# Expert pairs with a gate riding along: loading the gate weights in pair 2, its bases by column halves, side work handed out by products

## The chip, the cores and the metric

One core of a Trainium2 chip runs the program. The metric is the device time of one execution in microseconds (us), the median of several; smaller is better. Engines are named as in the profile: PE is TensorE (PEld its weight loads), DVE is VectorE, ACT is ScalarE, POOL is GpSimd and SP is SyncE, which here only issues DMAs.

## The reference, cut to what matters

Two blocks run one after the other on 512 rows of 1024 numbers. The change lies in the end of the second one, an expert layer in which each of 16 experts takes its own best rows, and a gate that reads the sum which the experts leave in x:

```python
def expert_choice_ffn(h, w_router, w_gate, w_up, w_down):
    cap = EC_CAPACITY * S // N_EXPERTS                 # 64 rows for each expert
    aff = softmax(h @ w_router)
    gates, idx = lax.top_k(aff.transpose(0, 2, 1), cap)
    xe = h[bidx, idx]
    a = einsum('becd,edf->becf', xe, w_gate)
    b = einsum('becd,edf->becf', xe, w_up)
    ye = einsum('becf,efd->becd', silu(a) * b, w_down)
    return zeros_like(h).at[bidx, idx].add(ye * gates[..., None])

x = x + expert_choice_ffn(rms_norm(x, norm_ffn), w_router, w_gate, w_up, w_down)
g = sigmoid(rms_norm(x, norm_ple) @ w_ple_gate)
e = rms_norm(p @ w_ple_proj, norm_ple_post)
x = x + g * e
```

Each expert's three weights are 1024 by 2048 in float32, 24 MB, so 384 MB go through the core in this stage.

## The kernel before, in words

**Pairs and slots.** Experts go two at a time, one in each half of the PE array: eight pairs, 0 to 7, from about 1030 us to the end. Weights come in chunks of 1 MB (128 by 2048), 48 for a pair and 384 in all, in the order in which PE uses them. A pair is cut into 24 slots of two chunks. A slot is eight matmuls on 64 columns, each of which the profile shows as two records. Slots 0 to 15 make gate and up in four sections (ga, ua, L1698 and L1699), slots 16 to 23 the down product (yd, L1728 and L1729). I write slot 4.2 for slot 2 of pair 4.

**Buffers.** A chunk waits for a free buffer; SP issues its load (L1292) in order, so a load that waits holds all behind it. Buffers come from five groups: chy (5) and x16 (2) serve to the end, chr (6) until the pair RETIRE, chl (3) until the pair E_AT. From pair RETIRE on there are thus seven.

**Side work.** Beside the slots runs work that has its own small lists. `todo` holds generators, and `between()`, called behind each slot, lets `meanwhile(n)` take n steps from it, where n comes from the table PACE (1.9 steps a slot in pairs 3 to 5, say). The generators are:

- `spread`: adds the two experts' output into x, a scatter for each of four row tiles and two column halves (po<-ys, L1538; x is the tile xk in the trace, the add is L1646).
- `embedding` (pair E_AT = 1): loads w_pp and pT into two chr buffers (L1577, L1578) and makes p @ w_ple_proj, eight tiles of two products (pe).
- `gate_base(t, h)`: the gate's product of what x holds at that time, for row tile t and column half h: eight transposes (ptg), then eight products (pg) with the gate weights. A product is one call of `halves`, two matmuls.
- `gate_pair`: adds to the gate what a pair adds to x later. It makes the product of the pair's outputs with the gate weights (z, eight products for each column half that has a base), splits it in two (zs, by ACT and DVE, L333 and L334), and scatters it into those tiles of g that had a base by then (po<-zs).

So the later a tile gets its base, the fewer scatters follow, and a column half needs z only from its first base on. BASE lists the pair in which each base is made: t0, t1 for h0 in pair 3, t2, t3 in pair 4, t0, t1 for h1 in pair 5, then one in pair 6 and one in pair 7. All bases of a pair must have read x before the pair's own output goes into it (L1741); as generators they stand behind the pair before's spread.

**Gate weights.** `ple_loads()` runs when pair RETIRE begins: four loads of 1 MB on SP into chr buffers (L1564), and eight scalings on POOL (L1566).

**Routing of the next pair.** `route` has its own list: a matmul (bc, L1470), DVE operations, a gather of the next pair's rows by POOL (xg, L1478), a copy of the gate factors (gs on POOL, L1484), a scaling of the rows (xg on ACT, L1486), and transposes (pxt). `between` advances it by half a step a slot.

**Order.** A scheduler orders each engine's instructions by priorities; from pair HOLD = 4 on, what `between` hands out is pinned behind the last matmul of its slot (`issue_after`). Before that it may be moved.

Of the kernel before, what the change touches and what calls it, by code (L numbers as in the profile page):

```python
# [27 lines left out]
XV = 4  # L28
ADA_N = 1
PO = 10  # L30
PACE = [1.0, 1.0, 1.0, 1.9, 1.9, 1.9, 2.1, 2.2]
ROUTE_PACE = 0.5
HOLD = 4
ADDPE = [1, 3, 5, 6]
TBK = 7
RETIRE = 3

BASE = {3: [(0, 0), (1, 0)], 4: [(2, 0), (3, 0)], 5: [(0, 1), (1, 1)], 6: [(2, 1)], 7: [(3, 1)]}
E_AT = 1
ADA0 = 0  # L40
ADA_EVERY = 3
# [188 lines left out]
def _build(ctx, tc, nc, a, dbg, stop):  # L230
# [9 lines left out]
    def bcast(src, n, parts=128, off=0):  # L240
        return bass.AP(tensor=src.tensor, offset=src.offset + off, ap=[[0, parts], [1, n]])
# [15 lines left out]
    def ps(name, tag, bufs, shape=(128, 512)):  # L257
        tag = tag[1:] if tag[0] == "=" else TG[0].get(name, tag)
        return psp.tile(list(shape), FT, name=name, tag=tag, bufs=bufs)
# [1015 lines left out]
    for p_ in range(8):  # L1275
# [9 lines left out]
        BUFS = {"chy": 5, "chr": 6, "chl": 3, "hts": 1, "yy": 2, "x16": 2}  # L1285
    UNTIL = {"x16": 48 * 8, "chy": 48 * 8, "chr": 48 * RETIRE, "chl": 48 * E_AT}
    first = ["chy"] * 5 + ["chr"] * 2 + ["hts"] + ["chr"] * 4 + ["x16"] * 2 + ["chl"] * 3 + ["yy"] * 2
# [212 lines left out]
    todo = []  # L1500

    def meanwhile(n=1):
        while todo and n:
            try:
                next(todo[0])
                n -= 1
            except StopIteration:
                todo.pop(0)

    todo.append(first_route())  # L1510
    meanwhile(ROUTE0)
# [12 lines left out]
    def s2k(name, shape=(128, S)):  # L1524
        return mp.tile(list(shape), FT, name=name, tag="sg", bufs=2)

    def hl(src, y):
        split(src, y[:, 0], y[:, 1])
        return y

    def yy(name):
        return mp.tile([128, 2, 2, S], FR, name=name, tag="yy", bufs=2)
# [17 lines left out]
    def halves(out, w, x_, start, stop):  # L1550

        for h in range(2):
            c_ = slice(64 * h, 64 * h + 64)
            T.matmul(out[c_], w[:, c_], x_, start=start, stop=stop)  # L1554

    def slot(tag):
        return pools[tag].tile([128, 2048], FT, name="ch", tag=tag, bufs=BUFS[tag])
# [12 lines left out]
    def embedding():  # L1570

        e = ple["e"] = [t[:, D * i:D * i + D] for t in (slot("chl"), slot("chl")) for i in range(2)]
        rest = slot("chl")
        gpost, ple["xf"] = rest[:, 0:D], rest[:, D:].rearrange("p (f c) -> p f c", f=8)
        P.dma_start(gpost, bcast(a["g_post"], D))
        wpp, pT = slot("chr").rearrange("p (k c) -> p k c", k=2), slot("chr")
        SY.dma_start(wpp, a["w_pp"][0].rearrange("p (k c) -> p k c", k=2))  # L1577
        SY.dma_start(pT[:, 0:1024], a["pT"])  # L1578
        pT = pT[:, 0:1024].rearrange("p (k c) -> p k c", k=2)
        yield  # L1580
        se = mp.tile([128, 8], FT, name="se")
        for t in range(4):
            for h in range(2):
                c_ = slice(S * h, S * h + S)
                pe_ = ps("pe", "o", 2)
                for k in range(2):
                    halves(pe_, pT[:, k, 128 * t:128 * t + 128], wpp[:, k, c_], k == 0, k == 1)
                V.tensor_copy(e[t][:, c_], pe_)
                A.activation(s2k("sq"), pe_, AF.Square, accum_out=se[:, 2 * t + h:2 * t + h + 1])
                yield  # L1590
        re_ = mp.tile([128, 4], FT, name="re_")
        tc.keep_in_program_order(A.preload_act_table_set(LN_EXP))
        rstd_parts(se, re_, 2)
        for t in range(4):
            V.scalar_tensor_tensor(e[t], e[t], re_[:, t:t + 1], gpost, op0=OP.mult, op1=OP.mult)
# [18 lines left out]
    def gate_pair(pr, yts, ott, zl):  # L1614

        hs = [h for h in range(2) if any(c[1] == h for p_, l in BASE.items() if p_ <= pr for c in l)]
        zl += [ps("z", "o", 2) for _ in hs]
        at = [(n, y) for n, c in enumerate((4, 4) if pr < 7 else (4, 2, 2)) for y in range(c)]
        left = [list(range(8)) if h in hs else [] for h in range(2)]
        while left[0] or left[1]:  # L1620

            ready = [h for h in range(2) if left[h] and at[left[h][0]][0] < len(yts)]
            if ready:
                h = ready[0] if pr == 7 else max(ready, key=lambda h: (len(left[h]), -h))
                k = left[h].pop(0)
                halves(zl[h], yts[at[k][0]][:, at[k][1]], ple["wg"][k // 2][:, k % 2, S * h:S * h + S], k == 0, k == 7)
            whole[:] = [not l for l in left] if pr == 7 else whole
            yield
        if pr == 7:
            return  # L1630
        zs = yy("zs")
        for h in hs:
            y = hl(zl[h], zs[:, h])
            yield
            for t in range(4):
                if snap.get((t, h), 8) <= pr:
                    g_ = ple["g"][t][:, S * h:S * h + S]
                    V.tensor_tensor(g_, g_, scatter(y, ott, t), op=OP.add)
                    yield

    def spread(y, ott, q):

        yield
        for t in range(4):
            x_ = xt[:, t, S * q:S * q + S]
            V.tensor_tensor(x_, x_, scatter(y, ott, t), op=OP.add)  # L1646
            yield

    snap, pairs, whole = {}, [0], [False, False]
    owed, way = [0.0], [0.0]  # L1650

    def between(last):

        owed[0] += PACE[pairs[0]]
        n = int(owed[0])
        owed[0] -= n
        with ExitStack() as c_:
            if pairs[0] >= HOLD:
                c_.enter_context(tc.issue_after(last.ins))
            way[0] += ROUTE_PACE  # L1660
            if way[0] >= 1 and (pairs[0] or not todo):
                way[0] -= 1
                on_the_way()
            meanwhile(n)

    sx = mp.tile([128, 12], FT, name="sx")
    for pr in range(8):
# [5 lines left out]
        if pr < 7:  # L1673
            ways.append(route(pr + 1))
        if pr == RETIRE:
            ple_loads()
        if pr == E_AT:
            todo.append(embedding())
        todo += [gate_base(*c) for c in BASE.get(pr, ())]
        hts, flip = None, []  # L1680
# [34 lines left out]
        _, gs, ott = routed.pop(pr)  # L1715
        ys, yts, z = yy("ys"), [], []
        if pr >= min(BASE):
            todo.append(gate_pair(pr, yts, ott, z))
        for q in range(2):
            parts = 2 if last and q else 1  # L1720
            n = S // parts
            for part in range(parts):
# [10 lines left out]
                y = hl(yg, ys[:, q, :, n * part:n * part + n])  # L1733
                if pr >= min(BASE):
                    pt = ps("pty", "pt", 2)[:, 0:n]
# [4 lines left out]
                    yts.append(yt)  # L1740
                while any(c not in snap for c in BASE.get(pr, ())):  # L1741
                    meanwhile()
# [15 lines left out]
    for h in range(2):  # L1758
# [5 lines left out]
        for t in range(4):  # L1764
            c_, n = slice(S * h, S * h + S), 4 * h + t
# [35 lines left out]
```

## Time and profile before

| | us |
|---|---|
| median of three runs | 2066.95 (2062.79 to 2067.37) |
| the profiled execution | 2067.67 |
| its span in the trace | 2065.9 |
| PE busy | 1944.7 (94%) |
| first matmul of pair 1, 2 | 1133.60, 1259.40 |
| last matmul of pair 2, first of pair 3 | 1379.58, 1400.54 |
| first matmul of pair 4, 5, 6, 7 | 1515.30, 1640.70, 1774.15, 1899.17 |
| end of pair 7's slots | 2028.0 |

Starts count from the beginning of the span. The page gives busy shares in 40 slices of 51.6 us each; "windows" give the same for stretches that one names: start and end, length, then busy time (and instructions) of PE, PEld, DVE, ACT and POOL, PE's granted clock as a share of 2.4 GHz, the mean busy share of the DMA engines, and GB/s. In a "timeline" each line is one instruction or a run of like ones: start, length, engine, line, operation, tiles, and in square brackets the idle time of the engine before it and what ended it. "Lines" group instructions: busy time, mean ns of one record.

### The profile page before, as it was taken

The page shows a single profiled execution, that of the slowest core. Times are in us where ns is not written, and L with a number is a line of the kernel's source. Part 1 is how long each engine was busy: PE and PEld are TensorE (multiplying, and loading weights), DVE is VectorE, ACT ScalarE, POOL GpSimd, SP SyncE. Part 2 cuts the span into 40 slices and gives each one's busy share as a digit, 9 for nine tenths or more (in the row PEclk, how much of TensorE's full clock was granted, in tenths as well). Part 3 has the DMA queues.
Part 4 walks back from the last instruction along what each step waited for, and adds up shares of the span by engine and source line. Part 5 has one row for each costly group of instructions (what it writes and reads, how often), then busy time and mean ns, then how long its engine had stood idle before and what let it go on. Part 6 is the DMA issues. An engine that isn't in the chain of part 4 may idle for free.

```text
span 2065.9 us, 23336 instructions
## 1 busy us (share of the span) xinstructions
PE 1944.7 (94%) x9084; PEld 1090.8 (53%) x9084; DVE 769.5 (37%) x1662; ACT 591.2 (29%) x1144; POOL 126.8 (6%) x127
## 2 busy tenths in 40 slices
PE   7989999989999998999899988779899999999998
PEld 4667667768888887777533322222334333333333
DVE  4767767764444346766431111010011111120212
ACT  4755656643333334454211110000000000100013
POOL 1210201300100000001000000020000000000000
PEclk9999989989999999999899999999999999999999
DMA  7432213432322231223889899999999999999991
GB/s 307 124 122 78 93 62 123 138 92 92 122 102 93 102 114 55 92 77 110 343 354 420 357 419 420 420 420 399 421 419 416 410 384 388 393 403 410 412 379 47
DMA packets 94191, 523.20 MB, mean 253 GB/s; under 512 B 11405, under 2 KB 11829, under 8 KB 43136
## 3 DMA queue, kind: packets, MB, share of 16 engines
q1 hardware_dynamic: 88832, 500.47, 61.7%
q0 software_dynamic: 3904, 18.88, 2.4%
q10 hardware_dynamic: 1344, 2.35, 0.3%
q8 instruction: 72, 1.18, 0.2%
q14 instruction: 39, 0.32, 0.0%
HBM read 510.31 MB, written 4.27 MB: 249 GB/s over the span
## 4 chain that ended last, share of the span: by engine, by line
PE 76%; DMA 13%; DVE 5%; ACT 3%; issue 2%; POOL 1%; DVEq 0%; POOLq 0%; SPq 0%; ACTq 0%
DMA ch<-in_w_ue_dram 6%; PE ua L1698 6%; PE ga L1699 5%; PE ga L1698 5%; PE yd L1729 4%; PE yd L1728 4%; DMA ch<-in_w_de_dram 4%; PE z L1554 3%; PE pg L1554 3%; PE od L653 2%; PE ua L1699 2%; PE po L1538 2%; PE ag L328 2%; PE ag L329 2%; PE ag L330 2%
## 5 line engine op out<-in xcount | busy, mean ns | idle before, releaser
L1699 PE MATMUL ua<-ch,xe 128*64 128x512 f32 x512 | 231.0, 595 | 14.4 <-DMA ch<-in_w_ue_dram 14.4
L1729 PE MATMUL yd<-ch,hts 128*64 128x512 f32 (+1 forms) x544 | 232.8, 576 | 11.1 <-DMA ch<-in_w_de_dram 11.1
L1698 PE MATMUL ga<-ch,xe 128*64 128x512 f32 x512 | 240.8, 605 | 0.0
L1699 PE MATMUL ga<-ch,xe 128*64 128x512 f32 x512 | 234.1, 602 | 1.9 <-DMA ch<-in_w_ge_dram 1.8
L1728 PE MATMUL yd<-ch,hts 128*64 128x512 f32 (+1 forms) x544 | 233.9, 577 | 0.0
L1698 PE MATMUL ua<-ch,xe 128*64 128x512 f32 x512 | 233.2, 595 | 0.0
L321 DVE TENSOR_TENSOR wlo<-pan,whi 128x1024 fp32r<-128x1024 f32 x119 | 147.8, 1242 | 161.4 <-ACT whi L318 159.1
L318 ACT ACTIVATE whi<-pan 128x1024 fp32r<-128x1024 f32 x119 | 125.8, 1057 | 201.9 <-PE ag L329 85.4
L1709 DVE TENSOR_TENSOR sg<-sg,ua 128x512 f32<-128x512 f32 x32 | 22.0, 687 | 283.8 <-PE ua L1699 283.8
L1729 PEld LDWEIGHTS yd<-ch,hts 128*64 128x64 f32 x544 | 72.8, 138 | 88.7 <-issue 63.8
L1699 PEld LDWEIGHTS ga<-ch,xe 128*64 128x64 f32 x512 | 66.8, 138 | 89.4 <-issue 82.0
L1698 PEld LDWEIGHTS ua<-ch,xe 128*64 128x64 f32 x512 | 67.3, 137 | 85.9 <-issue 84.5
L1728 PEld LDWEIGHTS yd<-ch,hts 128*64 128x64 f32 x544 | 72.2, 138 | 66.0 <-issue 64.3
L1699 PEld LDWEIGHTS ua<-ch,xe 128*64 128x64 f32 x512 | 67.3, 137 | 68.8 <-issue 42.4
L356 POOL TENSOR_TENSOR ada_a<-ada_a,adw 128x512 f32<-128x512 f32 x56 | 79.2, 1415 | 377.7 <-ACT ada_a L353 269.0
L334 DVE TENSOR_TENSOR ys<-yg,ys 128x512 fp32r<-128x512 f32 (+1 forms) x17 | 12.5, 736 | 222.6 <-ACT ys L333 222.6
L1698 PEld LDWEIGHTS ga<-ch,xe 128*64 128x64 f32 x512 | 65.9, 138 | 55.3 <-issue 54.0
L1688 ACT ACTIVATE hts<-pth 128x512 f32<-128x512 f32 x32 | 19.1, 596 | 265.5 <-PE pth L1687 265.5
L1732 ACT ACTIVATE yg<-yd,gs 128x512 f32<-128x512 f32 (+1 forms) x17 | 11.3, 662 | 277.8 <-PE yd L1729 210.1
L1708 ACT ACTIVATE sg<-ga 128x512 f32<-128x512 f32 x32 | 19.1, 597 | 209.8 <-PE ga L1699 209.8
L1554 PE MATMUL pg<-ch 128*64 128x512 f32 x256 | 76.8, 613 | 2.4 <-POOL ch L1566 2.4
L328 PE MATMUL ag<-hTh,whi 128*128 128x512 f32 x176 | 70.9, 403 | 2.2 <-ACT hTh L425 2.2
(902 smaller groups left out, 3739.3 us busy)
## 6 DMA issues: line engine op xcount, KB each, us to landing
ch<-in_w_de_dram SPq DMA_DIRECT2D x128, 1024.0 KB, 11.6
ch<-in_w_ue_dram SPq DMA_DIRECT2D x125, 1024.0 KB, 11.4
ch<-in_w_ge_dram SPq DMA_DIRECT2D x120, 1024.0 KB, 11.1
pan<-in_w_up_dram SPq DMA_DIRECT2D x44, 512.0 KB, 3.4
adw<-in_ada_dram SPq DMA_DIRECT2D x64, 256.0 KB, 2.7
pan<-in_w_in_dram SPq DMA_DIRECT2D x24, 512.0 KB, 3.7
pan<-in_w_dn_dram SPq DMA_DIRECT2D x22, 512.0 KB, 3.4
adr<-in_ada_dram SPq DMA_DIRECT2D x8, 1024.0 KB, 10.6
```

Of the source, the lines that this page charges most:

```text
L318: A.activation(hi, raw, AF.Copy)
L321: eng.tensor_tensor(lo, raw, hi.bitcast(FT), op=OP.subtract)
L328: T.matmul(out, wh, xh, start=first, stop=False)
L329: T.matmul(out, wh, xl, start=False, stop=False)
L330: T.matmul(out, wl, xh, start=False, stop=last)
L356: P.tensor_tensor(ada_next[1], ada_next[1], w, op=OP.add)
L653: T.matmul(acc_[64 * par:64 * par + 64, 128 * i:128 * i + 128], v(kb, par)[:w], p_[par][:w, 128 * kb:128 * kb + 128], start=start and kb = ...
L1554: T.matmul(out[c_], w[:, c_], x_, start=start, stop=stop)
L1698: T.matmul(acc_[m][0:64], xe[:, kk, 0:64], wa[:, k], start=kk == 0, stop=kk == 7)
L1699: mm = T.matmul(acc_[m][64:128], xe[:, kk, 64:128], wb[:, k], start=kk == 0, stop=kk == 7)
L1728: T.matmul(yd[0:64], hts[:, kk, 0:64], wa[:, k_], start=kk == 0, stop=kk == 15)
L1729: mm = T.matmul(yd[64:128], hts[:, kk, 64:128], wb[:, k_], start=kk == 0, stop=kk == 15)
```

## The change

Four things. RETIRE goes from 3 to 2, so the gate weights load when pair 2 begins. BASE is spread over pairs 2 to 7: two h0 bases in pair 2, two in pair 3, then one h1 base in each of pairs 4 to 7. The steps get weights: a tile of the embedding counts 2, a product 1, a scatter 0.5, and a `gate_pair` step that finds nothing ready counts 0 and ends the handing out for that slot. The table PACE is replaced by a number computed for each pair: its products divided by 23, with 14 more in pair 7.

```diff
-PACE = [1.0, 1.0, 1.0, 1.9, 1.9, 1.9, 2.1, 2.2]
+PACE0 = [1.0, 1.0]
-RETIRE = 3
+RETIRE = 2
-BASE = {3: [(0, 0), (1, 0)], 4: [(2, 0), (3, 0)], 5: [(0, 1), (1, 1)], 6: [(2, 1)], 7: [(3, 1)]}
+BASE = {2: [(0, 0), (1, 0)], 3: [(2, 0), (3, 0)], 4: [(0, 1)], 5: [(1, 1)], 6: [(2, 1)], 7: [(3, 1)]}
     def meanwhile(n=1):
-        while todo and n:
+        while todo and n > 0:
             try:
-                next(todo[0])
-                n -= 1
+                c = next(todo[0])
+                if c == 0:
+                    return 0
+                n -= 1 if c is None else c
             except StopIteration:
                 todo.pop(0)
+        return min(n, 0)
...
+    pace = list(PACE0)
+    for p_ in range(len(PACE0), 8):
+        made = [c for q_, l in BASE.items() if q_ < p_ for c in l]
+        n = 9.0 * len(BASE.get(p_, ())) + 5.0 + 9.0 * len({h for _, h in made}) + 0.5 * len(made)
+        pace.append((n + (14.0 if p_ == 7 else 1.0)) / 23)
...
-        owed[0] += PACE[pairs[0]]
-        n = int(owed[0])
-        owed[0] -= n
+        owed[0] += pace[pairs[0]]
...
-            meanwhile(n)
+            owed[0] = meanwhile(owed[0])
```

The yields become `yield 2` in `embedding`, `yield 1 if ready else 0` in `gate_pair`'s products, and `yield 0.5` in its scatters and in `spread`.

On SP, in the loads of pair 1, this is the order before (w_pp and pT are the embedding's, the rest are chunks):

```order
L1292 DMA ch<-in_w_ge_dram 128x2048 x4
L1292 DMA ch<-in_w_ue_dram 128x2048 x4
L1292 DMA ch<-in_w_ge_dram 128x2048 x4
L1292 DMA ch<-in_w_ue_dram 128x2048 x2
L1577 DMA ch<-in_w_pp_dram 128x2048
L1578 DMA ch<-in_pT_dram 128x1024
L1292 DMA ch<-in_w_ue_dram 128x2048 x2
```

And on SP in the same place after, beginning with the same chunks:

```order
L1292 DMA ch<-in_w_ge_dram 128x2048 x4
L1292 DMA ch<-in_w_ue_dram 128x2048 x2
L1581 DMA ch<-in_w_pp_dram 128x2048
L1582 DMA ch<-in_pT_dram 128x1024
L1292 DMA ch<-in_w_ue_dram 128x2048 x2
```

The two loads have moved eight chunks forward; the pe products (not shown) go from slots 1.6 to 1.11 to slots 1.2 to 1.10.

On POOL, the scalings of the gate weights (L1566) and the routing of the pair that follows (L1478, L1484) before, between pairs 2 and 3:

```order
L1566 TENSOR_TENSOR ch<-ch,cols 128x1024 x2
L1478 DMA xg<-xd,at 128x1056
L1566 TENSOR_TENSOR ch<-ch,cols 128x1024 x2
L1484 COPY gs<-xg 64x1 x2
L1566 TENSOR_TENSOR ch<-ch,cols 128x1024 x4
```

And on POOL after, now between pairs 1 and 2:

```order
L1570 TENSOR_TENSOR ch<-ch,cols 128x1024 x4
L1478 DMA xg<-xd,at 128x1056
L1570 TENSOR_TENSOR ch<-ch,cols 128x1024 x4
L1484 COPY gs<-xg 64x1 x2
L1478 DMA xg<-xd,at 128x1056
```

The last four scalings no longer stand behind the copy that waits for the gather. On PE the base that needs them still stands whole between the two pairs (eight ptg, 15 pg of 16 ahead of pair 2's first ga).

On ACT, at the beginning of pair 4, between two sections (sg is a section's activation, hts the transposed result, zs the split of pair 3's z, xg the scaling of the next pair's rows), before:

```order
L1708 ACTIVATE sg<-ga 128x512
L333 ACTIVATE zs<-z 128x512
L1486 ACTIVATE xg<-xg 128x1024
L1688 ACTIVATE hts<-pth 128x512
L1708 ACTIVATE sg<-ga 128x512
```

And on ACT in the same place after:

```order
L1716 ACTIVATE sg<-ga 128x512
L1486 ACTIVATE xg<-xg 128x1024
L333 ACTIVATE zs<-z 128x512
L1696 ACTIVATE hts<-pth 128x512
L1716 ACTIVATE sg<-ga 128x512
```

zs now stands behind xg. In pair 3 it does too; before, pair 3 had no zs. In pair 5 xg stands ahead of zs in both; there PE's first scatter of zs comes after slot 5.3 before, and after slot 5.7 now.

## Rows read from the trace of the kernel before

**Rows 1.** The page, part 2: DMA busy tenths and GB/s in 40 slices.

```profile
DMA  7432213432322231223889899999999999999991
GB/s 307 124 122 78 93 62 123 138 92 92 122 102 93 102 114 55 92 77 110 343 354 420 357 419 420 420 420 399 421 419 416 410 384 388 393 403 410 412 379 47
```

**Rows 2.** Windows: pair 2, the stretch to pair 3, then pairs 3 to 7.

```profile
1259.40:1379.58 120.18, 97.60 (x427) 33.10 (x424) 12.40 (x21) 8.45 (x13) 1.25 (x3) 1.00 1.01 420
1379.58:1400.54 20.96, 15.46 (x48) 5.58 (x50) 4.64 (x5) 3.55 (x5) 15.68 (x11) 0.76 1.01 419
1400.54:1515.30 114.76, 102.83 (x476) 36.06 (x472) 6.81 (x10) 8.47 (x14) 0.00 (x0) 1.00 0.99 411
1515.30:1640.70 125.40, 124.51 (x550) 46.71 (x549) 16.80 (x28) 11.16 (x19) 1.36 (x3) 1.00 1.01 414
1640.70:1774.15 133.45, 129.30 (x565) 45.96 (x564) 18.62 (x30) 11.27 (x19) 1.32 (x3) 0.97 0.96 388
1774.15:1899.17 125.02, 125.02 (x554) 43.30 (x553) 18.70 (x30) 10.61 (x17) 1.32 (x3) 1.00 0.99 404
1899.17:2028.00 128.83, 128.06 (x618) 50.13 (x619) 22.27 (x37) 15.43 (x34) 0.00 (x0) 1.00 0.88 358
```

**Rows 3.** Timeline of PE: two neighbouring matmuls of a slot; one scatter; two scatters.

```profile
1655.83 0.59 PE L1698 MATMUL ua<-ch,xe 128*64 128x512 f32 x1
1656.26 0.59 PE L1698 MATMUL ua<-ch,xe 128*64 128x512 f32 x1
...
1529.66 0.73 PE L1538 MATMUL po<-zs,ott 128*128 128x512 f32 x2
...
1539.90 1.20 PE L1538 MATMUL po<-ys,ott 128*128 128x512 f32 x4
```

**Rows 4.** Lines of PE in pair 6: z and ptg.

```profile
L1554 PE MATMUL z<-ch,yt 128*64 128x512 f32 x68 | 19.4, 594 | 0.0
...
L1604 PE MATMUL ptg<-cst,xk 128*128 128x128 f32 x8 | 1.1, 280 | 0.0
```

**Rows 5.** Timeline of POOL, then PE, between pairs 2 and 3.

```profile
1378.69 3.75 POOL L1566 TENSOR_TENSOR ch<-ch,cols 128x1024 f32<-128x1024 f32 x2 [117.69 <-DMA ch<-in_w_pg_dram]
1382.59 1.27 POOL L1478 DMA_INDIRECT xg<-xd,at  x1 [0.15 <-issue]
1383.88 3.75 POOL L1566 TENSOR_TENSOR ch<-ch,cols 128x1024 f32<-128x1024 f32 x2
1391.63 0.42 POOL L1484 COPY gs<-xg 64x1 f32<-64x1 f32 x2 [4.00 <-DMA xg<-xd,at]
1392.12 7.45 POOL L1566 TENSOR_TENSOR ch<-ch,cols 128x1024 f32<-128x1024 f32 x4
...
1397.77 2.93 PE L1554 MATMUL pg<-ch 128*64 128x512 f32 x8 [0.17 <-POOL ch L1566]
```

**Rows 6.** Timeline of SP in pair 1: a load that waits for its buffer.

```profile
1160.57 26.93 SPq L1292 DMA_DIRECT2D ch<-in_w_ue_dram  x4
```

**Rows 7.** Timeline of PE, POOL, ACT at pair 5's beginning, in order of time.

```profile
1649.45 0.39 PE L1470 MATMUL bc<-slots,two 16*128 16x512 bf16 x1
...
1652.33 0.96 POOL L1478 DMA_INDIRECT xg<-xd,at  x1 [115.14 <-DVE at L1476]
...
1661.03 1.15 ACT L1486 ACTIVATE xg<-xg 128x1024 f32<-128x1024 f32 x1 [10.88 <-DMA xg<-xd,at]
1662.09 0.58 ACT L333 ACTIVATE zs<-z 128x512 fp32r<-128x512 f32 x1
...
1662.72 2.37 PE L1538 MATMUL po<-zs,ott 128*128 128x512 f32 x4 [4.15 <-ACT zs L333]
```

**Rows 8.** Windows: in pair 1, in pair 5 and in pair 7.

```profile
1180.00:1190.00 10.00, 10.00 (x46) 3.20 (x44) 1.63 (x3) 1.97 (x5) 0.00 (x0) 1.00 0.28 97
1660.00:1680.00 20.00, 17.28 (x58) 6.30 (x60) 4.63 (x7) 2.83 (x4) 0.36 (x2) 0.83 0.86 346
1980.00:2000.00 20.00, 20.00 (x96) 6.86 (x93) 1.38 (x2) 1.88 (x2) 0.00 (x0) 1.00 0.92 353
```

More of the change, by code (lines that the diff above doesn't have):

```diff
@@ L1589, in embedding @@
                 A.activation(s2k("sq"), pe_, AF.Square, accum_out=se[:, 2 * t + h:2 * t + h + 1])
-                yield
+                yield 2
         re_ = mp.tile([128, 4], FT, name="re_")
@@ L1627, in gate_pair @@
             whole[:] = [not l for l in left] if pr == 7 else whole
-            yield
+            yield 1 if ready else 0
         if pr == 7:
@@ L1633, in gate_pair @@
             y = hl(zl[h], zs[:, h])
-            yield
+            yield 0.5
             for t in range(4):
@@ L1638, in gate_pair @@
                     V.tensor_tensor(g_, g_, scatter(y, ott, t), op=OP.add)
-                    yield
+                    yield 0.5
     def spread(y, ott, q):
-        yield
+        yield 0.5
         for t in range(4):
@@ L1646, in spread @@
             V.tensor_tensor(x_, x_, scatter(y, ott, t), op=OP.add)
-            yield
+            yield 0.5
+    pace = list(PACE0)
[3 more added lines that the diff above has]
+        pace.append((n + (14.0 if p_ == 7 else 1.0)) / 23)
     snap, pairs, whole = {}, [0], [False, False]
```

## The prediction

> **What bounds the kernel now.** I read the page's slices first: from about 1050 us the DMA engines move some 420 GB/s until 1550 us, then mostly 384 to 412 [rows 1]. So this stage has two limits, and the windows by pair say where each holds. At 420 GB/s a chunk of 1 MB (1.0486 million bytes) takes 2.50 us and a pair's 48 take 119.8. Pair 2 lasts 120.18 us with PE busy for 97.60 of them: DMA sets it. Pairs 4 to 7 have PE busy for all but 0.9, 4.2, 0 and 0.8 us: there PE sets the time, and the DMA share falls to 0.88 at the end [rows 2]. Pair 3 is DMA's again. The 20.96 us ahead of it belong to nobody's main work [rows 2]: PE makes the first base there, at clock 0.76, waiting for POOL's scalings.
>
> For PE what counts is the amount of work in a pair. Two neighbouring matmuls of a slot start 0.43 us apart [rows 3]; eight of them on each of 24 slots are 82.4 us. The rest is side work: a z or pg matmul is 0.43 too, a scatter 0.60 to 0.73 [rows 3], say 0.65, eight ptg 1.2 with their start [rows 4].
>
> One long wait lies inside a PE-bound pair. In pair 5, bc is at 1649.45, the gather is issued at 1652.33, ACT starts on its rows at 1661.03, zs follows at 1662.09 because it is queued behind xg, and PE, out of matmuls, waits 4.15 us for zs: 13.27 us from bc to the scatter [rows 7]. Right behind it the granted clock is 0.83 over 20 us [rows 8], which at a half clock (1.2 GHz) for 17% of the stretch is 3.4 us more.
>
> **Part 1: embedding eight chunks earlier.** In pair 1, SP's row of 26.93 us is a load that waits for a buffer [rows 6]; DMA runs dry, 0.28 busy for 10 us, 7.2 us lost [rows 8]. The buffer is that of a chunk which PE releases with slot 1.9. After, the same load waits for the same slot, two chr buffers are gone eight chunks earlier, and 28 of the 32 pe matmuls stand ahead of that slot instead of 17: it comes later by 11 x 0.43 = 4.7 us. But two earlier loads now wait too (for slots 1.2 and 1.3), so part of that idling is only moved. By adding the slots up I get three gaps of 1.7, 6.2 and 1.3 = 9.2 us against 7.2, so some 2 us lost, in a stretch that DMA sets. Bounds: 0 (all moved) and 6 (the 4.7 and 1.3).
>
> **Part 2: gate weights and first base to the boundary of pairs 1 and 2.** The four loads (4 x 2.50 = 10.0 us) and the eight scalings move; none is added. The block was 20.96 us. In it POOL waited 4.00 us for the gather ahead of gs, with four scalings of 7.45 us behind it [rows 5]. These no longer stand behind gs. Then POOL's chain is 3.75 + 1.27 + 3.75 + 7.45 = 16.2 us from 1378.69, thus over at 1394.9 instead of 1399.6, and the base's last matmuls follow it by 1.1 us, as at 1400.7 before: the block takes some 17.5 us. What SP queues behind: pair 2's chunks, which now find seven buffers instead of thirteen. That costs nothing while DMA sets the pace, but for the moments when all seven are full; before, that cost pair 3 (DMA 0.99 instead of 1.01, 411 GB/s [rows 2]) some 2 us.
>
> So pair 2 starts at 1259.4 + 2 + 17.5 = 1278.9 (before 1259.4), and now is what pair 3 was: seven buffers right behind the block, nearly the same PE work (by counting, 102.9 us against 102.5). Pair 3 took 114.76 [rows 2]. The block is 3.5 us shorter, so one chunk and a half fewer wait ready at its end, and the 2 us of full buffers mostly go: 114.8 + 3.5 - 2 = 116.3. Pair 3 starts at **1395.2**, 5.3 us earlier than the 1400.54 of before.
>
> **Part 3: pair 3.** It now has z (16 matmuls), ten scatters, two bases (16 ptg, 32 pg): to the number what pair 4 had. Pair 4 took 125.40 [rows 2]. But pair 3's zs stands behind xg on ACT as in pair 5. Between bc and the first scatter lie 24 matmuls, 10.3 us, so 13.27 - 10.3 = 3.0 us of wait; PE enters this pair with chunks just landing, and 1 us of it covers waits for those: 2. Pair 4 starts at 1395.2 + 125.4 + 2 = **1522.6** (before 1515.3).
>
> **Part 4: pair 4.** Against its own 125.40: z 18 for 16 (+0.9), twelve scatters for ten (+1.3), one base fewer (-1.2 - 16 x 0.43 = -8.1): 119.5. Its zs now stands behind xg; it didn't. The stretch from bc to the first scatter is that of pair 5 before, two products and two slots, so I take pair 5's wait, 4.15, and its clock, 3.4. DMA fills buffers meanwhile, which takes back the 0.9 us that PE idled in this pair and a little more: -1.5. 119.5 + 6.1 = 125.6: pair 5 starts at **1648.2** (before 1640.7).
>
> **Part 5: pairs 5 to 7.** Pair 5 loses its wait and its low clock (-7.6): its scatters of zs now come after slot 5.7. z 36 for 22 (+6.0), one scatter (+0.65), one base fewer (-8.1): 133.45 - 9.05 = 124.4, to **1772.6**. Pair 6: z 32 for 34, 125.02 - 0.9 = 124.1, to **1896.7** (before 1899.17). Pair 7: one product more (+0.9), and its side work ends in slot 7.12 instead of 7.16. From there a slot takes 3.43 us and its two chunks 5.0, so that four slots more live from the seven buffers: 4 x 1.57 = 6.3, less the turn's transposes, 1.6, which moved there too. DMA has room in that stretch (0.92, 353 GB/s [rows 8]): full buffers cover about half, and I take 2.5, bounds 0 and 4.7. 128.83 + 3.4 = 132.2: end at 2028.9 against 2028.0.
>
> **Sum:** +0.9 us on the profiled execution (2067.67), itself 0.7 above the median of 2066.95. That is 2068.6 by the one and 2067.9 by the other; I say **2068**, no change. The extra 16 products of the evener spread and the 7 us that pair 5 gains back nearly cancel, because the same wait appears in pairs 3 and 4.
>
> **Rivals.**
> (A) The gathers arrive in time. Then pairs 3 and 4 lose neither 2 nor 6.1 us: 2068 - 8 = 2060. For it: a gather's length isn't fixed, and pair 4 of before ran without a wait. Against it: there zs stood ahead of xg; the order now is that of pair 5. It decides at 8.6 us from bc to the rows' scaling in pair 4 (the cover of two products and two slots); the row shows 11.58 [rows 7]. The half-way case, the wait without the low clock, gives 2064.6.
> (B) Slower: SP's queue in pair 1. If the two earlier waits aren't made up, every microsecond by which slot 1.9 is late is lost to DMA in a DMA-bound pair: 6 instead of 2, and if PE, waiting for the chunks behind, makes that slot later still by the first two gaps (1.7), some 8: 2068 + 6 = 2074. It decides at whether the chunk behind the first gap lands before its slot needs it. For it: 26.93 us in SP's row, already the longest hole of the stage.
> (C) Waits in pair 3 pull the clock too: PE idles 3 us there, and if that brings a half clock as in pair 5 it costs 3.4: 2071.4. Against it: in pair 2 PE idled 22.6 us, in pieces, at clock 1.00 [rows 2]; for it, pair 5 at 0.83 [rows 8].
> The Trainium skill (TensorE: Matmul & The Clock Gate, section on HAM oscillation) says that matmul groups held apart by waits for data can each start again at the low clock; by that, C would hold in pair 3 and the time be 2071.4. The trace agrees in pair 5 and not in pair 2, so I give it little.
> (D) It doesn't even anything out: the first base still stands whole between two pairs, so what is spread is products from pair 3 on alone. That is in the sum already; if the scheduler bunches pair 3 as well, where nothing is pinned, another 3 us of block: 2071.
>
> **How the numbers follow.** The forecast 0.44, A 0.22 (a third of it as the half-way case), B 0.16, C 0.10, D 0.08. Measurements of this kernel tell 0.3%, 6.2 us, from no change: faster is below 2060.7, slower above 2073.2. A's full case gives most of faster; the forecast's own spread (parts 1, 3, 4 and 5 are each known to 2 or 3 us, so some 5 together) reaches either bound about one time in eight: faster 0.20, same 0.59, slower 0.21. The range takes in A and B: 2058 to 2076.
>
> **What would show it.** The first matmul of pair 2 near 1279, of pair 3 near 1395, of pair 4 near 1522, of pair 5 near 1648, of pair 6 near 1772, of pair 7 near 1897. A PE wait for zs of 2 us in pair 3 and 4 us in pair 4, the latter with a clock below 0.9 in the 20 us behind it, and none in pair 5. In pair 1, DMA gaps of 9 us together. A pair 4 that ends before 1643 would speak for A, a pair 2 that starts after 1282 for B. The prediction is wrong if pair 2 with its seven buffers takes much more than 116 us, since nothing in the trace of before shows a pair with the embedding's late chunks and the gate's loads on one another's heels.

## The result, and the profile after

The changed kernel takes 2080.05 us (median of 4, 2078.91 to 2080.66) against 2065.62 us of the kernel before in the same comparison: a ratio of 1.0068, 95% interval 1.0055 to 1.0081. That is 14.4 us slower, and 12 us above the forecast of 2068, outside its range. The profiled execution took 2078.91 us, its span is 2077.1.

The windows by pair of the changed kernel, with the columns of [rows 2]: pair 1 to its last matmul, the stretch between pairs 1 and 2, then pairs 2 to 7.

```profile
1132.56:1264.37 131.81, 113.72 (x492) 38.03 (x488) 22.06 (x33) 15.32 (x32) 1.80 (x3) 0.99 0.91 374
1264.37:1282.95 18.58, 15.23 (x50) 6.03 (x51) 5.61 (x10) 3.57 (x5) 15.34 (x11) 0.72 1.01 420
1282.95:1399.99 117.04, 103.77 (x483) 37.53 (x481) 9.09 (x15) 9.92 (x16) 0.00 (x0) 1.00 1.01 416
1399.99:1529.76 129.77, 121.06 (x546) 42.92 (x542) 14.69 (x24) 11.23 (x18) 1.36 (x3) 1.00 0.96 385
1529.76:1655.07 125.31, 119.31 (x516) 42.08 (x515) 17.27 (x29) 10.14 (x17) 1.33 (x3) 0.97 1.00 409
1655.07:1783.24 128.17, 127.32 (x556) 44.13 (x556) 19.47 (x31) 10.75 (x18) 1.32 (x3) 1.00 1.00 407
1783.24:1907.55 124.31, 124.00 (x550) 44.22 (x549) 19.33 (x31) 10.84 (x17) 1.32 (x3) 1.00 1.00 403
1907.55:2040.25 132.70, 129.06 (x626) 50.26 (x627) 21.57 (x36) 15.42 (x33) 0.00 (x0) 1.00 0.87 354
```

The last column is the one to read. The bytes are the same in both kernels, and DMA moves some 421 GB/s when it has a free buffer. So a stretch's **DMA idle time** is its length times (1 - GB/s / 421), and whatever idles is added to the end. Between the first matmuls of the pairs (some are moved ahead of the pair, so the borders differ from the windows' by a few us), and for pair 7 to its last down product, it comes to:

| DMA idle time, us | pair 0 | 1 | 2 | 3 | 4 | 5 | 6 | 7 | sum | time of the profiled execution less sum |
|---|---|---|---|---|---|---|---|---|---|---|
| before | 8.5 | 8.2 | 0.3 | 2.9 | 2.0 | 10.6 | 5.0 | 19.4 | 56.9 | 2011 |
| changed | 7.7 | 14.6 | 1.2 | 11.2 | 3.7 | 4.4 | 5.3 | 20.9 | 69.0 | 2010 |

The sums differ by 12.1 us, the two profiled executions by 11.2 and the medians by 14.4. Pair 1 gives 6.4 of the 12.1, pair 3 8.3; pair 5 takes 6.2 back. This is bookkeeping: with the same bytes, time less idle time has to come out nearly the same. It tells where the time went and not why; in pair 7, say, DMA idles because PE is the slower one.

In pair 1, windows of 20 us of the changed kernel (before, they had 419, 419, 250 and 423 GB/s: one hole where there are now three), and SP's two waiting loads where [rows 6] had one:

```profile
1130.00:1150.00 20.00, 18.02 (x78) 6.00 (x76) 3.36 (x5) 2.47 (x3) 0.43 (x2) 1.00 0.83 342
1150.00:1170.00 20.00, 19.84 (x88) 6.83 (x86) 4.14 (x6) 3.15 (x8) 0.00 (x0) 1.00 0.66 259
1170.00:1190.00 20.00, 17.58 (x86) 6.27 (x84) 3.46 (x5) 2.46 (x6) 0.00 (x0) 1.00 1.01 421
1190.00:1210.00 20.00, 16.42 (x74) 5.25 (x72) 1.38 (x2) 2.46 (x6) 0.00 (x0) 1.00 0.88 357
```

```profile
1130.17 29.18 SPq L1292 DMA_DIRECT2D ch<-in_w_ge_dram  x4
...
1169.69 23.21 SPq L1292 DMA_DIRECT2D ch<-in_w_ue_dram  x4
```

In pair 3, windows of the changed kernel. DMA falls to 306 and 340 GB/s in the middle, as it would if all seven buffers were full, and at the end it runs at 421 while PE is busy for 18.21 of 20:

```profile
1430.00:1450.00 20.00, 19.69 (x85) 6.94 (x84) 2.77 (x5) 1.78 (x3) 0.00 (x0) 1.00 0.79 306
1450.00:1470.00 20.00, 19.11 (x90) 7.31 (x88) 2.76 (x4) 1.20 (x2) 0.00 (x0) 1.00 0.90 340
...
1510.00:1530.00 20.00, 18.21 (x86) 6.32 (x88) 1.14 (x3) 1.32 (x2) 0.00 (x0) 1.00 1.01 421
```

In pairs 3 and 4, the timeline of PE and ACT where PE waits for zs, in order of time: what [rows 7] showed for pair 5 now stands in both.

```profile
1410.16 1.15 ACT L1486 ACTIVATE xg<-xg 128x1024 f32<-128x1024 f32 x1 [12.47 <-DMA xg<-xd,at]
1411.21 0.58 ACT L333 ACTIVATE zs<-z 128x512 fp32r<-128x512 f32 x1
...
1411.85 0.50 PE L1542 MATMUL po<-zs,ott 128*128 128x512 f32 x1 [2.25 <-ACT zs L333]
...
1538.49 0.38 PE L1470 MATMUL bc<-slots,two 16*128 16x512 bf16 x1
...
1551.45 1.15 ACT L1486 ACTIVATE xg<-xg 128x1024 f32<-128x1024 f32 x1 [12.25 <-DMA xg<-xd,at]
1552.50 0.58 ACT L333 ACTIVATE zs<-z 128x512 fp32r<-128x512 f32 x1
...
1553.13 1.52 PE L1542 MATMUL po<-zs,ott 128*128 128x512 f32 x2 [5.11 <-ACT zs L333]
```

And the granted clock in the windows that hold these two waits (the column before DMA's share): it stays at 1.00 behind the first and falls behind the second.

```profile
1410.00:1430.00 20.00, 16.87 (x66) 6.08 (x67) 5.22 (x8) 2.72 (x4) 0.36 (x2) 1.00 1.01 415
...
1550.00:1570.00 20.00, 16.87 (x60) 5.80 (x60) 3.95 (x6) 2.83 (x4) 0.36 (x2) 0.83 0.99 396
```

And PE's products of the first base, in the block between pairs 1 and 2: all in one row, with no wait for POOL in front of it.

```profile
1274.08 9.09 PE L1558 MATMUL pg<-ch 128*64 128x512 f32 x32
```

### The profile page after: what moved, and what is told of

The parts are those of the page before. It is cut to its first block, busy times and chain, and to the rows that moved or that the text cites. A ratio compares the mean times of both kernels' runs of the same rounds, so it can differ in the third digit from the quotient of the medians.

```text
span 2077.1 us, 23493 instructions
## 1 busy us (share of the span) xinstructions
PE 1961.8 (94%) x9166; PEld 1098.1 (53%) x9166; DVE 773.2 (37%) x1671; ACT 592.5 (29%) x1146; POOL 126.4 (6%) x127
## 4 chain that ended last, share of the span: by engine, by line
PE 81%; DMA 7%; DVE 6%; ACT 3%; issue 2%; POOL 0%; DVEq 0%; SPq 0%; POOLq 0%; ACTq 0%
PE ga L1707 6%; PE ua L1706 6%; PE yd L1737 5%; PE yd L1736 4%; PE ga L1706 4%; PE ua L1707 4%; PE z L1558 3%; PE pg L1558 3%; PE po L1542 2%; PE od L653 2%; DMA ch<-in_w_de_dram 2%; DMA ch<-in_w_ue_dram 2%; PE ag L328 2%; PE ag L329 2%; PE ag L330 2%
## 5 line engine op out<-in xcount | busy, mean ns | idle before, releaser
L1737 PE MATMUL yd<-ch,hts 128*64 128x512 f32 (+1 forms) x544 | 230.6, 572 | 10.6 <-DMA ch<-in_w_de_dram 10.5
L1558 PE MATMUL z<-ch,yt 128*64 128x512 f32 x320 | 98.5, 595 | 3.7 <-DVE yt L1747 3.7
## 6 DMA issues: line engine op xcount, KB each, us to landing
ch<-in_w_de_dram SPq DMA_DIRECT2D x128, 1024.0 KB, 10.6
ch<-in_w_ge_dram SPq DMA_DIRECT2D x120, 1024.0 KB, 10.6
```

The source lines that it names most:

```text
L1737: mm = T.matmul(yd[64:128], hts[:, kk, 64:128], wb[:, k_], start=kk == 0, stop=kk == 15)
```

## Experiments

Seventeen kernels. Each run's own median of the kernel before, on the same chip, was 2065.9 to 2067.5. The changed kernel is 2080. What each edit does to DMA's idle time in the pairs that matter is in the table behind them. The runs' windows begin at a pair's first matmul even where it is moved ahead, those of the changed kernel above begin behind such ones: for pair 3 that is 4.7 us, for pair 4 2.4, for pair 5 nothing.

### Which half of the change costs?

**Weights alone.** The changed kernel with the old RETIRE and BASE:

```diff
-RETIRE = 2
+RETIRE = 3
-BASE = {2: [(0, 0), (1, 0)], 3: [(2, 0), (3, 0)], 4: [(0, 1)], 5: [(1, 1)], 6: [(2, 1)], 7: [(3, 1)]}
+BASE = {3: [(0, 0), (1, 0)], 4: [(2, 0), (3, 0)], 5: [(0, 1), (1, 1)], 6: [(2, 1)], 7: [(3, 1)]}
```

> The changed kernel with RETIRE and BASE as before: only the weights of the steps and the computed pace are new. The order then has the embedding early in pair 1 as in the changed kernel, and zs behind xg in pair 4, not in pair 5. Theory (of the 14 us, some 6 come from the embedding's early loads in pair 1): pair 1 has 14 to 15 us of DMA idle time instead of 8.2, the wait for zs moves from pair 5 to pair 4 at the same price: about 2073. Rival (the loss is due to the moved bases): 2066 to 2068.

Measured 2073.8 (ratio to before 1.0047, 1.0030 to 1.0064). Pair 1 idles 14.5 us, the wait moves to pair 4, as the theory had it.

**Bases alone.** The kernel before with the new RETIRE and BASE:

```diff
-RETIRE = 3
+RETIRE = 2
-BASE = {3: [(0, 0), (1, 0)], 4: [(2, 0), (3, 0)], 5: [(0, 1), (1, 1)], 6: [(2, 1)], 7: [(3, 1)]}
+BASE = {2: [(0, 0), (1, 0)], 3: [(2, 0), (3, 0)], 4: [(0, 1)], 5: [(1, 1)], 6: [(2, 1)], 7: [(3, 1)]}
```

> The kernel before with RETIRE = 2 and BASE over pairs 2 to 7, the steps and the table of paces as before. The embedding then stands where it stood, no base stands whole between two pairs (the first goes to slots 2.4 to 2.7), and side work in pair 3 lasts to slot 3.19. Theory (the early embedding, the waits for zs and pair 3's bunched work cost the time, not the bases' new places): one wait for zs is left, in pair 3, where PE waits for chunks anyway; 2061 to 2067. Rival (the 16 products and five scatters added by the new BASE cost their 18 us where PE sets the time): 2073 or more.

Measured 2059.8 (0.9978, 0.9968 to 0.9987): faster than before by 6 us, although it has the same 16 products and five scatters more on PE as the changed kernel. The windows of its pairs 1, 3, 5 and 7:

```profile
1131.60:1265.90 134.30, 114.87 (x497) 38.74 (x493) 26.68 (x41) 18.26 (x35) 9.67 (x7) 0.96 0.96 396
1387.90:1518.30 130.40, 122.23 (x551) 44.13 (x549) 16.93 (x28) 11.12 (x18) 1.36 (x3) 1.00 0.98 399
1641.70:1765.00 123.30, 123.30 (x546) 44.01 (x545) 18.68 (x30) 10.63 (x17) 1.32 (x3) 1.00 1.01 420
1890.00:2019.20 129.20, 128.32 (x620) 51.05 (x621) 22.26 (x37) 15.42 (x33) 0.00 (x0) 1.00 0.88 356
```

Pair 5 runs at 420 GB/s in 123.30 us; in the changed kernel, with the same bases, it took 128.17. The weights change the counts too: in pair 5, z has 30 matmuls here and 36 in the changed kernel (x60 and x72 in the lines of PE), which is 2.6 us of the 4.9. So the moved bases gain 6 us, the weights with the computed paces lose 8, and together they lose 14: once the bases are moved the weights cost 20. They meet somewhere. That is what the next runs are for.

### Pair 1: the embedding's loads

**Old steps in pairs 0 and 1**, which puts the embedding back by eight chunks:

```diff
-                n -= 1 if c is None else c
+                n -= 1 if c is None or pairs[0] < 2 else c
```

> The changed kernel, but in pairs 0 and 1 every step of side work counts as one again, so that the embedding's two loads and products stand where they stood before, eight chunks later; all else as changed. Theory (the time was lost in pair 1, where DMA moved 342, 259 and 357 GB/s in three windows of 20 us against 419, 419 and 250 to 262 before): pair 1 gets back about 5.5 us and the changed kernel's 2080 becomes about 2074.5. Rival (later pairs are set by PE and absorb what DMA loses in pair 1): within 1.5 us of 2080.

Measured 2077.5 (2074.2 to 2083.9, 5 runs): between the two. The profiled execution, from which the rest is read, took 2081.3. Pair 1 does get its 6 us back (idle 8.4), and its last matmul ends 5.5 us earlier, at 1258.9. But pair 2 idles 5.8 us instead of 1.2 and pair 3 14.1 instead of 11.2. For pair 2 the trace shows why, in the block between the pairs: gs stands between the scalings again, PE waits for POOL, and DMA is left without work behind it, as it would be with all seven buffers full. Why pair 3 idles more isn't shown. PE's last products of the base in that run, and the window behind:

```profile
1277.13 3.83 PE L1558 MATMUL pg<-ch 128*64 128x512 f32 x8 [4.47 <-POOL ch L1570]
```

```profile
1280.00:1290.00 10.00, 10.00 (x42) 3.16 (x40) 0.69 (x1) 0.60 (x1) 0.00 (x0) 0.84 0.46 180
```

**The list of buffers.** `chunk()` picks the group whose oldest buffer is freed first, from the list `held`. The embedding takes two chr buffers and doesn't tell the list. Telling it (71 is about the chunk by which the products are done), first in the kernel before:

```diff
         wpp, pT = slot("chr").rearrange("p (k c) -> p k c", k=2), slot("chr")
+        held["chr"] = held["chr"][2:] + [71, 71]
```

> The kernel before with the same edit to the list of buffers alone. Theory: pair 1's DMA idle time falls from 8.2 us to 1 to 3; but the block of 21 us ahead of pair 3, in which PE stands still with seven buffers full, follows, so that 3 to 6 us remain of it: 2060 to 2063. Rival: within 1.5 us of before (2066).

Measured 2059.7 (0.9971, 0.9961 to 0.9981). Pair 1 idles 2.0 us instead of 8.2 and all of it is kept; I had expected the block to eat a part.

The same edit on the bases alone:

> The kernel with RETIRE and BASE alone (2059.8), and one edit: when the embedding takes two of the six chr buffers, the list by which chunks choose a group of buffers is told so, so that chunk 70 takes a buffer of another group. Theory (the load that waits 24 us on SP in pair 1 waits because the list doesn't know of the two buffers; DMA idles 7 us for it): pair 1's DMA idle time falls from 8.2 to 1 to 3 us and, pair 2 being set by DMA, some 5 us are gained, 2055. Rival (another load waits instead, since two buffers are missing): 2058 to 2061.

Measured 2054.2 (0.9951, 0.9934 to 0.9967). Pair 1 of that run, 415 GB/s where the bases alone had 396:

```profile
1128.80:1257.10 128.30, 111.27 (x497) 37.78 (x493) 26.70 (x41) 18.25 (x35) 9.50 (x7) 0.99 1.00 415
```

And in the changed kernel itself, with 69 for 71 since the products are done earlier:

> The changed kernel with the edit to the list of buffers alone (the early embedding's two buffers are taken off it). Theory (the loss of pair 1 has the list as its cause, and a gain in pair 1 is in part lost again in the block that follows): pair 1's DMA idle time falls from 14.6 us to 2 to 4, pairs 2 and 3 together idle 4 to 8 us more: 2072 to 2077. Rival (the early loads cost by themselves, two buffers being gone for longer): pair 1 stays above 10 us, 2078 to 2081.

Measured 2076.0. Pair 1 idles 8.6 us instead of 14.6, so the list is the cause of 6 us here too, and 8.6 is more than I expected: with the early loads some 6.6 us stay (8.6 less the 2.0 of the other two) that the list doesn't explain. They lie between 1150 and 1210 us (390, 321 and 379 GB/s in windows of 20 us); the longest row of SP there is one of 21.38 us in w_ge's loads from 1149.13. Which buffer it waits for stays open. Pair 3 idles 14.2 us instead of 11.2, the gain being lost again in part, as with the old steps.

### The waits for zs

**The scaling of the gathered rows on POOL**, so that zs isn't queued behind a gather on ACT:

```diff
-        A.activation(xg[:, 0:D], xg[:, 0:D], AF.Copy, scale=xg[:, D + 16:D + 17])
+        P.tensor_scalar(xg[:, 0:D], xg[:, 0:D], xg[:, D + 16:D + 17], None, op0=OP.mult)
```

> The changed kernel, but the scaling of the next pair's gathered rows (xg) goes from ACT to POOL, so that zs no longer stands behind the gather on ACT. Theory (the waits for zs cost): the waits of 2.25 us in pair 3 and 5.11 us in pair 4 vanish and with them the low clock behind the second (3.4 us); at most 10.8 us, but DMA was busy throughout pair 4 and sets it from 119.8 us on, so some 6 us: about 2074. Rival (DMA sets pairs 3 to 5 anyway): 2078 to 2080, with the waits gone from the trace and waits for chunks in their place.

Measured 2073.3. Both waits are gone, and in pairs 3 and 4 so is the low clock:

```profile
1395.80:1525.60 129.80, 122.19 (x551) 43.14 (x549) 16.94 (x28) 10.33 (x17) 4.23 (x4) 1.00 0.97 393
1525.60:1648.90 123.30, 120.45 (x527) 44.41 (x524) 17.34 (x29) 10.41 (x17) 4.21 (x4) 1.00 1.01 420
```

The same edit on the kernel before:

> The kernel before, with one edit: the scaling of the gathered rows (xg) on POOL instead of ACT. Theory (the wait of 4.15 us for zs in pair 5 and the half clock behind it are lost time also before): pair 5's DMA idle time of 10.6 us falls to about 5, so some 5.5 us faster than before, about 2061. Rival (the wait is covered: with it gone PE waits for chunks): 2065 to 2067.

Measured 2062.5 (0.9984, 0.9975 to 0.9994). Pair 5 idles 3.5 us instead of 10.6; pair 3 gives 2.2 us back.

### Pair 3: where the side work stands

**HOLD = 3** in the changed kernel, and the same line with 2 in the other run:

```diff
-HOLD = 4
+HOLD = 3
```

> The changed kernel, but with HOLD = 3: pair 3's side work is pinned behind its slots and so spread evenly, where the scheduler had moved it ahead (both bases' products by slot 3.15, none in 3.16 to 3.19). Theory (pair 3's bunching costs: DMA idles 6.2 us between 1430 and 1470 with full buffers, then PE waits for chunks at the pair's end): that idle time goes, but the wait for zs in pair 3 grows from 2.25 to some 4 us with a low clock behind it as in pair 4: net 0 to 5 us faster, 2075 to 2080. Rival (it is the amount of side work alone, not where it stands): 2080 to 2084, slower by the longer wait.

Measured 2079.0, within the theory's range but telling little: in pair 3 the wait for zs grew from 2.25 to 3.74 us and the clock fell behind it (0.83 in the window from 1410 to 1430 us), which hid the rest.

> As the one with HOLD = 3, but with HOLD = 2: pair 2's side work is pinned too, so that the first base no longer stands whole between pairs 1 and 2 (18.6 us in the changed kernel) but in slots 2.2 to 2.10. Theory (pair 2 is set by DMA, the block costs little because DMA goes on in it): within 3 us of the run with HOLD = 3. Rival (the block is PE time that is missing later, in pair 3, which starts with no chunk ready): 5 to 10 us faster than that run.

Measured 2081.2: the block is gone from between pairs 1 and 2, and nothing is gained. PE waits 8.46 us for the first chunk of pair 2 instead, since the gate weights are loaded ahead of it. So nothing shows that the block by itself cost time in the changed kernel: DMA moved 420 GB/s through it, and pair 2 idled 1.2 us. (This edit pins pair 3 too, where the wait for zs is now 3.41 us with a low clock behind it.)

**HOLD = 3 and the scaling on POOL** (both diffs above):

> The changed kernel with HOLD = 3 and the scaling of the gathered rows on POOL; the early embedding stays. Theory (with the wait for zs gone, pinning pair 3's side work shows what its bunching cost): pair 3's DMA idle time falls from 8.5 us (scaling on POOL alone) to about 3, so 2073.3 - 5.5 = 2068. Rival (bunching costs nothing, the amount of work does): 2072 to 2074.

Measured 2067.6, 5.7 us faster than with the scaling on POOL alone. Pair 3 idles 3.2 us instead of 8.5, and takes 4 us less:

```profile
1394.50:1520.30 125.80, 125.01 (x551) 43.94 (x549) 16.83 (x28) 10.29 (x17) 4.23 (x4) 1.00 1.01 410
```

So the place of the work in pair 3, not its amount, cost 5 us; without the wait for zs that can be seen, with it it can't.

**The same on the bases alone** (list of buffers, scaling on POOL, HOLD = 3; old steps and paces):

> The moved bases with the old steps and paces and the edit to the list of buffers (2054.2), with HOLD = 3 and the scaling on POOL besides. Theory (what is left of pair 3's DMA idle time, 7.8 us, is its side work being bunched where nothing is pinned): it falls to about 3 and some 4 us are gained, 2050. Rival (old steps pinned are as uneven): 2053 to 2056.

Measured 2050.2 (0.9921, 0.9904 to 0.9937), the lowest median here (the last run below is within noise of it), some 16 us below the kernel before. Pair 3 idles 2.9 us instead of 7.8; which of the two edits does it wasn't tried on this kernel.

### Do the causes add up?

Old steps in pairs 0 and 1 and the scaling on POOL:

> The changed kernel with steps of pairs 0 and 1 counting one each and the scaling on POOL, HOLD = 4 as changed, so that the first base stands whole between pairs 1 and 2. Theory (pair 1's 6 us of DMA are gained only where no block follows; here the block gives DMA more to idle for, as in the run with old steps, 5.8 us in pair 2's beginning): no more than 2 us better than the scaling alone, 2071 to 2074. Rival (pair 1's gain is kept once the waits for zs are gone): 2067.

Measured 2075.4, where the scaling alone had 2073.3: no gain, and a loss that isn't clear of noise. Pair 1 idles 10.3 us, but pair 2 6.4 and pair 3 10.4: the block eats it.

Old steps and HOLD = 2, without the scaling on POOL:

> The changed kernel with steps of pairs 0 and 1 counting one each and HOLD = 2, the scaling on ACT as changed. Theory (each alone gave nothing, 2077.5 and 2081.2, since the block ate the first and the second had nothing to keep): pair 1 idles 8.3 us and pairs 2 and 3 no more than with HOLD = 2 alone, so the 6 us are kept: 2073 to 2076; what is left to 2059.9 is the wait for zs in pairs 3 and 4 with its low clock. Rival: 2077 or more, the three causes don't add up.

Measured 2071.3. Pair 1 idles 8.1, pair 2 0.3: now it is kept. Alone, old steps had gained 2.6 and HOLD = 2 had lost 1.1.

All three (old steps, HOLD = 2, scaling on POOL):

> The changed kernel with three edits at once: steps of pairs 0 and 1 count one each, HOLD = 2, and the scaling of the gathered rows on POOL. Theory (three causes that add up: pair 1's loads 6 us, waits for zs and the low clock 6 to 7 us, bunched work in pair 3 some 5 us): each only shows when the others are gone, since the first was eaten by the block between pairs 1 and 2 in the run with old steps, and the third by a longer wait in the run with HOLD = 3; all gone, about 2062. Rival (they are one and the same slack, or PE's added work is the limit): 2068 to 2074, no better than the run with the scaling on POOL alone (2073.3) by more than 5 us.

Measured 2059.9 (0.9972, 0.9962 to 0.9983), and with the list of buffers too:

> The kernel with three edits (old steps in pairs 0 and 1, HOLD = 2, scaling on POOL: 2059.9) and the edit to the list of buffers. Theory: pair 1 idles 2 us instead of 8.3 and keeps it, about 2054, no better than the moved bases with the old paces and that edit (2054.2): the weights of the steps bring nothing by themselves. Rival (weighted steps spread the work better): 2050 or less.

Measured 2054.2. So with three causes and their chain removed, 20 us go, more than the changed kernel had lost. That isn't a split of its 14: the scaling on POOL gains 3.4 in the kernel before too, and HOLD = 2 wasn't tried on that one. The weighted steps then only reach what the old steps reach with the list alone (2054.2), and stay behind those with HOLD = 3 and the scaling on POOL as well (2050.2).

### The computed paces in pairs 4, 5 and 7

On the kernel just named:

```diff
-        pace.append((n + (14.0 if p_ == 7 else 1.0)) / 23)
+        pace.append((n + {4: 14.0, 7: 4.0}.get(p_, 1.0)) / 23)
```

> The kernel with old steps in pairs 0 and 1, HOLD = 2, scaling on POOL and the edit to the list (2054.2), with other numbers in the computed pace: 14 added in pair 4 instead of 1, so that six of its z matmuls come in its own last slots and not in pair 5, and 4 added in pair 7 instead of 14, so that its side work lasts to slot 7.15 and not 7.12. Theory (the computed paces cost pair 5 some 5 us and pair 7 some 3.7: these last 128.2 and 132.9 in every run with weighted steps, 123.2 and 129.1 in the runs with the old table): pair 5 falls to about 126 (four of the six z matmuls are moved, 1.7 us) and pair 7 to 129 or 130, 2048 to 2051. Rival (it is the order of z and scatters, not the paces): 2053 to 2055.

Measured 2050.8. Its pairs 4, 5 and 7:

```profile
1506.30:1632.00 125.70, 121.50 (x533) 41.93 (x529) 17.40 (x29) 10.37 (x17) 4.21 (x4) 1.00 1.00 410
1632.00:1757.40 125.40, 124.54 (x550) 43.10 (x549) 19.36 (x31) 9.73 (x17) 4.21 (x4) 1.00 1.00 414
1881.70:2011.40 129.70, 128.59 (x624) 51.09 (x624) 21.64 (x36) 15.31 (x33) 0.00 (x0) 1.00 0.89 361
```

Pair 7 falls from 132.9 to 129.7: 14 added there instead of 4 cost 3.2 us. Pair 5 falls from 128.2 to 125.4, but pair 4 rises from 122.2 to 125.7: its side work now ends in slot 4.11 and it idles 3.3 us. So the number of z matmuls that come late moves pair 5's time (four fewer in it, 32 for 36), as I had it, but this edit only shifted the loss; that pair 5 can have 123.3 beside a pair 4 of 123.4 is shown by the bases alone.

### The table

DMA idle time in us, worked out as above; medians in us.

| kernel | pair 1 | pair 2 | pair 3 | pair 4 | pair 5 | pair 7 | sum (all pairs) | median |
|---|---|---|---|---|---|---|---|---|
| before | 8.2 | 0.3 | 2.9 | 2.0 | 10.6 | 19.4 | 56.9 | 2065.6 |
| changed | 14.6 | 1.2 | 11.2 | 3.7 | 4.4 | 20.9 | 69.0 | 2080.1 |
| weights alone | 14.5 | 0.3 | 2.6 | 8.4 | 3.5 | 20.5 | 64.2 | 2073.8 |
| bases alone | 8.2 | 1.1 | 6.8 | 1.4 | 0.4 | 19.6 | 50.1 | 2059.8 |
| changed, old steps in 0 and 1 | 8.4 | 5.8 | 14.1 | 3.4 | 3.8 | 22.4 | 71.9 | 2077.5 |
| changed, scaling on POOL | 14.7 | 1.1 | 8.5 | 0.3 | 4.1 | 21.7 | 62.8 | 2073.3 |
| changed, HOLD 3 and POOL | 14.5 | 1.3 | 3.2 | 0.3 | 4.3 | 21.3 | 58.2 | 2067.6 |
| changed, old steps, HOLD 2 and POOL | 8.3 | 0.2 | 3.0 | 0.3 | 4.4 | 21.2 | 50.1 | 2059.9 |
| the same and the list | 2.0 | 0.3 | 2.9 | 0.3 | 4.0 | 22.3 | 44.0 | 2054.2 |
| bases alone and the list | 2.0 | 1.0 | 7.8 | 1.2 | 0.3 | 19.6 | 42.8 | 2054.2 |
| the same, HOLD 3 and POOL | 2.0 | 0.8 | 2.9 | 2.3 | 0.3 | 19.6 | 40.3 | 2050.2 |

The idle times are those of the profiled execution, and that execution's time less the sum is 2007 to 2011 in every row. Two rows should not be held against their median: with old steps in pairs 0 and 1 the profiled execution took 2081.25, 3.8 above it, and with the bases alone and the list 2049.55, 4.6 below it.

## Why the prediction was wrong

**Part 1, pair 1: a step that failed, in size.** I took 2 us, with bounds of 0 and 6, because the two earlier waits would take over idling from the later one. Measured: 6.4 us more idle time. My three gaps of 1.7, 6.2 and 1.3 us were some 3.8, 7.7 and 3.0 (342, 259 and 357 GB/s over 20 us each). Rival B was this case, with 6 to 8 us, and got 0.16. What I hadn't looked into is why a load waits there at all: I took the wait as given, as that of two missing buffers, and the runs with the list show that 6 us of it, in the kernel before and in the changed one, come from the choice of the buffer.

**Part 2, the block: right in its time, not in what sets it.** It took 18.58 us where I said 17.5, and pair 2 117.04 where I said 116.3, from the analogy with the old pair 3. But I let POOL's chain end the block, and the trace shows no wait of PE for POOL in it: the 32 records of pg run in one row of 9.09 us. PE's own scatters and products fill it, at a granted clock of 0.72. And the working there gives 16.3 us and not 17.5 (20.96 less the 4.7 by which POOL ends earlier), so some of the agreement is luck.

**Part 3, pair 3: a step that failed, the analogy.** "To the number what pair 4 had": the numbers agree, but pair 4's work is pinned to its slots and pair 3's isn't (HOLD = 4). The order showed it: ptg and pg done by slot 3.15, none behind. I used the order for counts and not for places. Pair 3 took 129.8 us instead of 127.4, and in DMA's account idled 11.2 us where the old pair 4 idled 2.0. The wait for zs, 2.25 us, was 2 in the forecast. Two runs with POOL, with and without HOLD = 3, show the price of the place: 5.3 us of idle time, 5.7 us of time.

**Part 4, pair 4: right, in part by luck.** 125.3 us against 125.6; the wait was 5.11 us (forecast 4.15), the clock 0.83 over 20 us as in [rows 8]. The half clock lasts 6.8 us (1551.1 to 1557.9), 2.0 of them inside the wait, so it cost some 2.4 us here and not 3.4. I had charged 8.1 us for the waits of parts 3 and 4 together. With them gone (scaling on POOL), pairs 2 to 4 took 365.6 us instead of 372.1, 6.5 less, since DMA at 420 GB/s then sets pair 4.

**Part 5: pair 5 is the largest step that failed, pairs 6 and 7 right.** Pair 5 took 128.2 us instead of 124.4. I added PE's work up from the old pair 5, and that sum was too low: PE is busy for 127.3 us of the pair and idle for 0.85, so hardly any of the 3.8 is a wait that the trace shows. With the old table of paces, and the same bases, the pair took 123.3, but with six z matmuls fewer; with four fewer, in the last run, 125.4. So the z matmuls that the paces leave over from pair 4 are 2.6 of the 4.9 us between the two kernels. For the rest I have an explanation that no run isolates: PE begins this pair with hardly a chunk ahead, DMA runs at 420 GB/s for its first 70 us, and then bunched scatters (slots 5.7 to 5.12) fill the buffers, 349 and 367 GB/s from 1725 to 1745, so that the pair alternates between two limits. What makes the sum of PE's work 2.9 us too low stays open. Pair 6 was 124.3 (124.1), pair 7 132.7 (132.2), the latter with the mechanism as forecast, the side work's early end; the pace run measured it at 3.2 us.

**The sum and the range.** The errors by part are +3.0 (pair 1's end), +1.1, +0.7, +2.4, -0.3, +3.8, +0.2 and +0.5, together 11.4, none very large and nearly all of one sign. I had let them be independent. As I read it they aren't: each comes from adding up an engine's work where buffers couple two engines, so that unevenness which I leave out adds time. That is an argument and no run tests it. The closing sentence, that added products and the regained wait cancel, fails too where the wait doesn't come back: the bases alone have those added products, no wait for zs of more than a microsecond in any pair, and are 6 us faster than before.

**Rivals.** A didn't come: the gather took 12.96 us from bc to the scaling in pair 4. B came. C: the 2.25 us in pair 3 left the clock at 1.00, so it didn't come in this execution. It was close: behind waits of 1.95 us (old steps in pairs 0 and 1) and 2.10 us (the list) at the same place the clock is 0.83 over 10 us. The Trainium skill (TensorE: Matmul & The Clock Gate, section on HAM oscillation) tells of groups of matmuls that start again at the low clock behind waits for data, waits longer than this 2.25 us; the trace agrees behind the 5.11 us of pair 4 and the 3.74 us of pair 3 with HOLD = 3, and the two runs show a fall behind shorter ones. D, pair 3's bunching, came as well; I had priced it at 3 us, and it was 5.

## What to carry to other kernels

Where a stream of transfers feeds an engine through a few buffers, keep the account by the transfers' idle time, stretch by stretch: here a profiled execution's time less that sum was 2007 to 2011 us in all kernels of the table. It has to be, with the same bytes, and so it can't say why a stretch idles, but no loss escapes it, while my forecasts by adding up work were off by up to 4 us a pair. When a pair is costed by another one with the same counts, compare the places of the work as well, and whether the scheduler may move it. And a cost that disappears from one stretch isn't a gain until the stretch behind can use it: an edit that gave nothing alone (HOLD = 2) was what let the next one keep 6 us.

## What the runs showed that I had not expected

- Two buffers taken from a rotating group without telling the list that picks groups cost 6.2 us in the kernel before: one line gives 2059.7 instead of 2066.
- A block of 18.6 us in which PE does nothing for the pair cost DMA nothing ahead of a pair that DMA sets (420 GB/s through it), but where PE waits in it for POOL, 4.47 us, DMA loses 5.7 us of the ten behind (180 GB/s).
- Scaling 128 by 1024 numbers on POOL instead of ACT, next to the gather that POOL issues anyway, is worth 3.4 us in the kernel before and 6.7 in the changed one, though the scaling itself is slower there (2.85 us against 1.15).
- The clock isn't told by the length of a wait alone: 2.25 us left it at 1.00 in the changed kernel, 1.95 and 2.10 us at the same place were followed by 0.83 over 10 us.
